# A two-layer hybrid encoder on one core: joining two 256-column products into one of 512 columns in the input projection, evicting some tiles later, and scaling the scan's outputs by priority

## The chip, the cores and the metric

The kernel runs on 1 core of one Trainium2 chip. The metric is the device time of one execution in microseconds. TensorE (PE in the profile) multiplies matrices and its weight loads are listed as PEld; VectorE is DVE, ScalarE is ACT, GpSimd is POOL, and SyncE (SP) issues most DMAs.

## The reference

Two layers, each with an RMS norm, one input projection, two groups of heads and one output projection; 256 tokens, a model width of 2048, everything in f32.

```python
for l in range(DEPTH):
    h = rms_norm(x, norm_g[l])
    proj = jnp.einsum('btd,dc->btc', h, w_in[l])
    rw_in, g_rw, q, k_at, v_at, g_at = jnp.split(proj, col_splits, axis=-1)
    rw_in = bidir_token_shift(rw_in, shift_mu[l])
    r, k, v, xw, xa = jnp.split(rw_in, rw_splits, axis=-1)
    y_rw = rwkv7_branch(r, k, v, xw, xa, ...)      # 16 heads, a scan in each direction
    ...
    y_at = window_attention(qh, kh, vh, sink[l])   # 16 heads in groups of 4, window of 128
    mix = jnp.concatenate([y_rw * jax.nn.silu(g_rw), y_at * jax.nn.silu(g_at)], axis=-1)
    x = x + jnp.einsum('btc,cd->btd', mix, w_out[l])
return rms_norm(x, final_g)
```

## The kernel before

**The products.** Each f32 operand is split into a high and a low part, and a product is the sum of three: weights high by input high, weights high by input low, weights low by input high. `gemm` computes one output tile of 128 columns of the projection for all 256 tokens. It takes 16 steps, one for each 128 rows of the model width. In the input projection a step is three matmuls with 256 moving columns each (lines 332 to 334), all added up in one PSUM tile `pm`. In the output projection (all tiles but the last) it is two: high weights by the pair (high, low) of the input, which lie side by side as 512 columns, and low weights by the high part, 256 columns (lines 325 and 326). The two halves of the 512-column result are then added when the tile is evicted.

**The weights.** A tile's weights come in two halves of 8 steps. A half is loaded from HBM into one of three `raw` buffers, then split in two pieces of 512 columns: ACT copies to `hi` (line 254) and DVE subtracts to `lo` (line 256). There are two buffers of `hi` and of `lo`, so the split of the half after next waits until PE has read the last of the half before it.

**The order of the work.** `S` is a stream of such steps in a fixed order: per layer the values, two tiles of the low-rank inputs, then eight pairs of heads with four tiles each (k, v, r and gate), then attention's 18 tiles (two of keys, eight of queries, eight of gates), then 16 output tiles. `window(64, ...)` runs 64 steps, which is one pair, and between the steps places the stages of the scans of earlier pairs (`scan_p`, `scan_i`, `scan_b`) and, in the last three windows, attention. PE's instructions stand in the order in which the code writes them. For the other engines a scheduler lists them ahead of time, by priority (the place in the code, moved by `high_priority`) and by the time at which it expects the inputs; on the chip each engine then runs its list strictly in that order. Operations written with `PV` and `PA` keep their order among themselves on DVE and ACT; those written with `V` and `A` are free.

**What the change touches.** `inproj(ct, evac)` queues one tile of the input projection, and `evac` is called when its last step has been written. `S.later(n, f)` calls `f` n steps later. `shift_evac` (lines 473 to 482) evicts k, v and r: DVE multiplies `pm` by the norm's factors `rb` into `u`, and three more operations do the token shift. `silu_evac` (lines 484 to 492) evicts a gate through two tiles of the tag `g`. `rope_evac` copies `pm` to SBUF on ACT, turns it by four DMAs and rotates it on DVE. At the first step of a pair's k tile, `ups` (lines 578 to 584) takes two tiles of the same tag `g` for two small loads (`iu`, `du`); they are read 6 steps after the eviction of that pair's v tile, by `parts` (lines 589 to 595). These two are the only buffers with the tag `g`:

```python
g = st("g", [T], bufs=2)
th = st("g", [T], bufs=2)
```

The tiles `pm` have two PSUM banks, and a tile may use a bank when the last reader of the tile that held it is done:

```python
ps_main = pool("ps_main", 2, space=PSUM)
```

In `scan_b`, at the end of a pair's scan, ACT squares the outputs, DVE forms the variance `yv` (line 1080), POOL raises it to the power -1/2 (line 1081), and DVE scales the outputs `ysq` with it.

Of the kernel before, what the change touches and what calls it, by code (L numbers as in the profile page):

```python
# [21 lines left out]
T = 256  # L22
# [3 lines left out]
NP = 8  # L26
# [34 lines left out]
WARM = 11  # L61

# [72 lines left out]
def hybrid_trunk_kernel(ctx, tc, xT, wi, wv, wo, par, fing, dup, iup, sink, pos, cst, out):  # L135
# [80 lines left out]
    def x_split(XH, XL, x, k, l):  # L216
        g = G0[:, k : k + 1] if l == 0 else PR[:, l, P_NG + k : P_NG + k + 1]
        A.activation(XH[:, k, :], x, AF.Copy, scale=g)
        V.scalar_tensor_tensor(XL[:, k, :], x, g, XH[:, k, :].bitcast(F32), op0=ALU.mult, op1=ALU.subtract)
# [90 lines left out]
    def gemm(src, operands, evac, raws=None, begin=None, bank=None, pairs=None, wide=False):  # L310
# [3 lines left out]
        def step(kk):  # L314
            def f(w):
# [7 lines left out]
                if wide:  # L323
                    m = pairs()
# [3 lines left out]
                if pairs:  # L328
                    xh, xl = (pairs().row(kk, i) for i in range(2))
                else:  # L330
                    xh, xl = (x[:, kk, :] for x in operands())
# [133 lines left out]
    def queue_inputs(l):  # L465
# [4 lines left out]
        def inproj(ct, evac, **kw):  # L470
            gemm(wi[l, ct], lambda: (L.XH, L.XL), evac, **kw)

        def shift_evac(j, place):
            def evac(pm):
                dst = place()
                u = st("u", [T], bufs=2)
                V.tensor_tensor(u, pm, L.norm.rb, op=ALU.mult)  # L477
# [6 lines left out]
        def silu_evac(place):  # L484
            def evac(pm):
                g = st("g", [T], bufs=2)
                th = st("g", [T], bufs=2)
                V.tensor_tensor(g, pm, L.norm.rb, op=ALU.mult)
# [35 lines left out]
        def v_step(kk, b):  # L524
            def f(w):
# [5 lines left out]
                PE.matmul(pvs[b], L.XH[:, kk, tb], wh, start=(kk == 0), stop=False)  # L531
                PE.matmul(pvs[b], L.XH[:, kk, tb], wl, start=False, stop=False)
                PE.matmul(pvs[b], L.XL[:, kk, tb], wh, start=False, stop=(kk == 15))
# [69 lines left out]
        for p, t in enumerate(L.ts):  # L603
            inproj(2 + 4 * p, shift_evac(p, new(t, "k", "kr", 4)), begin=ups(p, t))
            inproj(3 + 4 * p, value_evac(p, t))
            inproj(4 + 4 * p, shift_evac(16 + p, new(t, "r", "kr", 4)))
            inproj(5 + 4 * p, silu_evac(new(t, "gr", "vg", 8)))
# [4 lines left out]
        def rope_evac(place):  # L612
            def evac(pm):
# [7 lines left out]
                A.activation(raw, pm, AF.Copy)  # L621
# [13 lines left out]
                S.later(13, turn)  # L635
                S.later(15, parts)
# [12 lines left out]
        for m in range(2):  # L649
            inproj(2 + 4 * NP + m, rope_evac(k_place(m)))  # L650
# [11 lines left out]
        for n in ("q0", "q1", "q2", "q3", "g0", "q4", "g1", "q5", "g2", "q6", "g3", "q7", "g4", "g5", "g6", "g7"):  # L662
            j = int(n[1])
            if n[0] == "q":
                inproj(QG0 + 2 * j, rope_evac(q_place(j)))
            else:
                inproj(QG0 + 2 * j + 1, silu_evac(new(L.tq[j], "g", "vg", 8)))

    def queue_output(l):
# [4 lines left out]
        def tile_of(k):  # L674
# [6 lines left out]
            def evac(pm):  # L681
# [32 lines left out]
        for k in range(NKT):  # L714
            ev, be = tile_of(k)
            gemm(wo[l, k], None, ev, begin=be, pairs=lambda: L.M, wide=k < NKT - 1)

    def layer(l):
# [3 lines left out]
        L.M = Pairs()  # L722
# [294 lines left out]
        def scan_b(p, t):  # L1017
# [65 lines left out]
            PV.tensor_tensor(ysq, py, yv.unsqueeze(2).to_broadcast([128, NC, 64]), op=ALU.mult)  # L1083
# [128 lines left out]
    L0.XH, L0.XL = Rows("s2", F32R, "XH"), Rows("s3", F32R, "XL")  # L1212
    for k in range(NKT):
        x_split(L0.XH, L0.XL, X0[:, k, :], k, 0)
# [117 lines left out]
```

## Time and profile before

| | |
|---|---|
| median of 3 runs | 1160.97 us (1160.34 to 1161.03) |
| the profiled execution | 1160.44 us, of which its span is 1158.6 us |
| windows of pairs 4 to 8, layer 1 | 120.32 to 317.95 us |
| windows of attention, layer 1 | 317.95 to 488.85 us |
| windows of pairs 4 to 8, layer 2 | 689.48 to 886.18 us |
| windows of attention, layer 2 | 886.18 to 1057.12 us |

The span runs from the first to the last instruction of the profiled execution; 1.8 us of its time lie outside. A row of the timeline gives start, duration, engine, line, operation, the tiles written and read, their shape and how many instructions it merges; in brackets stand the idle time of the engine before it and what ended it. A row of the windows gives, for a stretch of time, its length and the busy time of PE, PEld, DVE, ACT and POOL with their instructions, then the granted TensorE clock, the DMA share and GB/s.

### The profile page before, as it was taken

To read this page: it belongs to the slowest core of one execution; us is meant where nothing else is said; L and a number is where in the kernel's file an instruction comes from. 1 tells how busy PE (TensorE), PEld (TensorE's weight loads), DVE (VectorE), ACT (ScalarE), POOL (GpSimd) and SP (SyncE) were. 2 spreads that over 40 slices of the span, in tenths; PEclk is the share of its full clock that TensorE was granted. 3 is DMA by queue.
4 is the path that set the end of the run, shared out by engine and by line. 5 is a ranking of instruction groups with operands and counts; after the bars stand their busy time and mean duration, and the time that the engine had idled before them with its cause. 6 is when DMAs were issued, how large, how long until landed. Compare 5 with 4: busy or idle time off the path is not lost.

```text
span 1158.6 us, 37145 instructions
## 1 busy us (share of the span) xinstructions
PE 1139.9 (98%) x15659; PEld 1046.6 (90%) x15659; DVE 914.3 (79%) x2038; ACT 783.9 (68%) x1985; POOL 22.2 (2%) x23
## 2 busy tenths in 40 slices
PE   9999999999999999999999999999999999999996
PEld 7998999999999989888999899999999999898885
DVE  7899878878977768767767898888878866786665
ACT  7687767867776667655546678767867766675553
POOL 0000000000000000000000000000000000000000
PEclk9999999999999999999999999999999999999998
DMA  7553433333334343577755444333333443336663
GB/s 276 188 174 121 136 118 99 112 118 118 111 103 132 116 124 107 151 243 235 213 184 168 143 134 139 104 118 100 112 118 112 127 123 115 119 109 198 214 195 126
DMA packets 61878, 166.73 MB, mean 144 GB/s; under 512 B 9200, under 2 KB 24208, under 8 KB 61712
## 3 DMA queue, kind: packets, MB, share of 16 engines
q1 hardware_dynamic: 61424, 164.10, 45.6%
q8 instruction: 122, 2.00, 0.7%
q14 instruction: 44, 0.36, 0.1%
q10 hardware_dynamic: 288, 0.27, 0.1%
HBM read 157.27 MB, written 4.19 MB: 139 GB/s over the span
## 4 chain that ended last, share of the span: by engine, by line
PE 74%; issue 12%; DVE 6%; ACT 4%; DMA 3%; POOL 0%; SPq 0%; POOLq 0%; DVEq 0%; ACTq 0%
PE pm L332 16%; PE pm L333 14%; PE pm L334 13%; PE pm L325 4%; PE pg L877 3%; DVE lo L256 3%; PE pm L326 2%; PE pcc L1040 2%; DMA raw<-wi 2%; PE pcc L1068 1%; PE py L1052 1%; PE pd L984 1%; PE py L1025 1%; PE pcc L1058 1%; PE pq L975 1%
## 5 line engine op out<-in xcount | busy, mean ns | idle before, releaser
L254 ACT ACTIVATE hi<-raw 128x512 fp32r<-128x512 f32 x560 | 329.8, 625 | 171.8 <-PE pm L325 61.3
L256 DVE TENSOR_TENSOR lo<-raw,hi 128x512 fp32r<-128x512 f32 x560 | 371.9, 687 | 91.1 <-ACT hi L254 88.8
L332 PE MATMUL pm<-XHa,hi 128*128 128x256 f32 x832 | 245.4, 295 | 0.0
L332 PE MATMUL pm<-XHb,hi 128*128 128x256 f32 x832 | 242.7, 292 | 0.6 <-DVE u L477 0.6
L334 PE MATMUL pm<-XHa,lo 128*128 128x256 f32 x832 | 233.8, 281 | 1.1 <-DVE lo L256 0.6
L334 PE MATMUL pm<-XHb,lo 128*128 128x256 f32 x832 | 233.3, 280 | 0.6 <-DVE lo L256 0.6
L333 PE MATMUL pm<-XLa,hi 128*128 128x256 f32 x832 | 233.3, 280 | 0.0
L333 PE MATMUL pm<-XLb,hi 128*128 128x256 f32 x832 | 233.0, 280 | 0.0
L325 PE MATMUL pm<-M,hi 128*128 128x512 f32 x480 | 166.9, 392 | 0.1
L332 PEld LDWEIGHTS pm<-XHa,hi 128*128 128x128 f32 x832 | 156.5, 188 | 10.9 <-issue 2.2
L332 PEld LDWEIGHTS pm<-XHb,hi 128*128 128x128 f32 x832 | 156.5, 188 | 6.0 <-DVE u L477 0.8
L334 PEld LDWEIGHTS pm<-XHa,lo 128*128 128x128 f32 x832 | 156.6, 188 | 2.7 <-DVE lo L256 2.5
L334 PEld LDWEIGHTS pm<-XHb,lo 128*128 128x128 f32 x832 | 156.6, 188 | 1.3 <-DVE lo L256 1.1
L333 PEld LDWEIGHTS pm<-XLa,hi 128*128 128x128 f32 x832 | 156.7, 188 | 0.0
L333 PEld LDWEIGHTS pm<-XLb,hi 128*128 128x128 f32 x832 | 156.7, 188 | 0.0
L326 PE MATMUL pm<-M,lo 128*128 128x256 f32 x480 | 134.3, 280 | 0.2 <-DVE lo L256 0.2
L325 PEld LDWEIGHTS pm<-M,hi 128*128 128x128 f32 x480 | 90.1, 188 | 20.9 <-issue 0.8
L326 PEld LDWEIGHTS pm<-M,lo 128*128 128x128 f32 x480 | 90.1, 188 | 0.5 <-DVE lo L256 0.5
L1063 ACT ACTIVATE suv<-pcc 64x128 f32<-64x128 f32 x128 | 34.5, 269 | 66.1 <-PE pcc L1061 42.4
L978 ACT ACTIVATE QF<-pq 128x256 f16<-128x256 f32 x80 | 30.4, 380 | 10.8 <-PE pq L942 6.6
L877 PE MATMUL pg<-mv,FR 64*128 64x128 f32 x512 | 37.2, 285 | 0.0
L986 DVE CAST_PREDICATED tv<-LV,pd 128x256 f16<-128x256 uint8 x80 | 34.3, 429 | 3.3 <-PE pd L984 2.7
(282 smaller groups left out, 2034.8 us busy)
## 6 DMA issues: line engine op xcount, KB each, us to landing
raw<-wi SPq DMA_DIRECT2D x208, 512.0 KB
raw<-wo SPq DMA_DIRECT2D x64, 512.0 KB
raw<-wv SPq DMA_DIRECT2D x7, 512.0 KB
rrot<-u SPq DMA_DIRECT2D x80, 32.0 KB
vg<-xT SPq DMA_DIRECT2D x16, 128.0 KB
xd<-vg SPq DMA_DIRECT2D x16, 128.0 KB
vg<-xd SPq DMA_DIRECT2D x16, 128.0 KB
g<-dup SPq DMA_DIRECT2D x16, 97.0 KB
```

Source lines behind the costliest of these rows:

```text
L254: A.activation(hi[:, q], raw[:, q], AF.Copy)
L256: V.tensor_tensor(lo[:, q], raw[:, q], hi[:, q].bitcast(F32), op=ALU.subtract)
L325: PE.matmul(pm, wh, m.row(kk), start=(kk == 0), stop=(kk == 15), skip_group_check=True)
L326: PE.matmul(pm[:, 0:T], wl, m.row(kk, 0), start=False, stop=(kk == 15), skip_group_check=True)
L332: PE.matmul(pm, wh, xh, start=(kk == 0), stop=False)
L333: PE.matmul(pm, wh, xl, start=False, stop=False)
L334: PE.matmul(pm, wl, xh, start=False, stop=(kk == 15))
L877: PE.matmul(pg[:, h, c * 128 : (c + 1) * 128], BK[half[h], d, c, 1 - h : 3 - h, :].rearrange("p s j -> p (s j)"), MV[half[h], d, c].rearra ...
L978: A.activation(t_sub(QF), flat4(pq[:, :, 0:128]), AF.Copy)
L986: V.copy_predicated(t_sub(TC), t_mask, flat4(pd[:, :, 0:128]))
L1040: PE.matmul(pc[half[h], 0, d, :], GE[h][r, d, ci[d], 0, :], SUV[r, d, ci[d], h, :], start=True, stop=True)
L1063: A.activation(here(h), pc[half[h], 1], AF.Copy)
```

## The change

The inputs `X` are laid out as pairs (high, low) as the outputs' operand already was. Attention's 18 tiles and the tiles of the pairs from the fourth on (`WIDE = 3`, counted from 0) use the two-matmul step with a `pm` of 512 columns. Evicting such a tile starts with `scaled`: ACT copies one half of `pm`, DVE adds the other, and only then comes the multiplication by `rb`; `rope_evac` gets the addition alone. `LATE` gives the steps by which the eviction of such a tile is written later in the code: 3 for k, 0 for v, 0 for r, 2 for the gate, and by turns in attention. The scaling of the scan's outputs loses its place in the fixed order of `PV`.

```diff
+LATE = (3, 0, 0, 2)
+WIDE = 3
...
                 if wide:
-                    m = pairs()
+                    m = rows()
                     PE.matmul(pm, wh, m.row(kk), start=(kk == 0), stop=(kk == 15), skip_group_check=True)
                     PE.matmul(pm[:, 0:T], wl, m.row(kk, 0), start=False, stop=(kk == 15), skip_group_check=True)
                     return
...
-        def inproj(ct, evac, **kw):
-            gemm(wi[l, ct], lambda: (L.XH, L.XL), evac, **kw)
+        def inproj(ct, evac, late=0, **kw):
+            if late:
+                evac = lambda pm, evac=evac: S.later(late, lambda: evac(pm))
+            gemm(wi[l, ct], lambda: L.X, evac, **kw)
+
+        def scaled(o, pm):
+            x = pm
+            if pm.shape[-1] > T:
+                A.activation(o, pm[:, T : 2 * T], AF.Copy)
+                V.tensor_tensor(o, o, pm[:, 0:T], op=ALU.add)
+                x = o
+            V.tensor_tensor(o, x, L.norm.rb, op=ALU.mult)
...
-                V.tensor_tensor(u, pm, L.norm.rb, op=ALU.mult)
+                scaled(u, pm)
...
-                V.tensor_tensor(g, pm, L.norm.rb, op=ALU.mult)
+                scaled(g, pm)
...
-            inproj(2 + 4 * p, shift_evac(p, new(t, "k", "kr", 4)), begin=ups(p, t))
+            inproj(2 + 4 * p, shift_evac(p, new(t, "k", "kr", 4)), begin=ups(p, t), wide=p >= WIDE, late=LATE[0] if p >= WIDE else 0)
...
-                A.activation(raw, pm, AF.Copy)
+                A.activation(raw, pm[:, T : 2 * T], AF.Copy)
+                V.tensor_tensor(raw, raw, pm[:, 0:T], op=ALU.add)
...
-                S.later(13, turn)
-                S.later(15, parts)
+                S.later(13 - late, turn)
+                S.later(15 - late, parts)
...
-            PV.tensor_tensor(ysq, py, yv.unsqueeze(2).to_broadcast([128, NC, 64]), op=ALU.mult)
+            V.tensor_tensor(ysq, py, yv.unsqueeze(2).to_broadcast([128, NC, 64]), op=ALU.mult)
```

The order of the instructions is shown at three places, all in the window of the seventh pair of layer 1; the fifth, sixth and eighth pair and layer 2 have the same pattern. Line numbers of the changed kernel are 8 to 17 higher.

PE where the k tile ends and the v tile begins, before (`pm_4523` is k, `pm_4706` is v):

```order
L332 MATMUL pm_4523<-XHb_133,hi_4609 128x256
L333 MATMUL pm_4523<-XLb_135,hi_4609 128x256
L334 MATMUL pm_4523<-XHb_133,lo_4610 128x256
L332 MATMUL pm_4706<-XHa_132,hi_4688 128x256
L333 MATMUL pm_4706<-XLa_134,hi_4688 128x256
L334 MATMUL pm_4706<-XHa_132,lo_4689 128x256
```

and now (`pm_4347` is k, `pm_4516` is v):

```order
L333 MATMUL pm_4347<-X3_135,hi_4435 128x512
L334 MATMUL pm_4347<-X3_135,lo_4436 128x256
L333 MATMUL pm_4347<-X3_135,hi_4435 128x512
L334 MATMUL pm_4347<-X3_135,lo_4436 128x256
L333 MATMUL pm_4516<-X0_132,hi_4506 128x512
```

In both, v's first matmul stands right behind k's last, with nothing of the scans between; each step has one matmul fewer now. On ACT, k's eviction now stands between the two pieces of a split:

```order
L262 ACTIVATE hi_4630<-raw_4628 128x512
L483 ACTIVATE u_4613<-pm_4347 128x256
L262 ACTIVATE hi_4630<-raw_4628 128x512
L1059 ACTIVATE rh_4524<-pcc_4519 128x128
L493 ACTIVATE kr_4612<-u_4613,DP_103 128x256
```

where before ACT had no reader of `pm` there, and both pieces stood together:

```order
L254 ACTIVATE hi_4818<-raw_4816 128x512 x2
L1042 ACTIVATE rh_4715<-pcc_4710 128x128
L478 ACTIVATE kr_4700<-u_4701,DP_103 128x256
L1000 ACTIVATE q16_4774<-pf_4721 128x512
L946 ACTIVATE tt_3776<-pf_4721 128x2x4x32
```

The copy of k's second half moved in behind the first piece of the split of v's second half.

DVE where v has ended and r begins, before:

```order
L1080 TENSOR_SCALAR yv_4909<-yv_4909 128x4
L269 TENSOR_TENSOR th_4445<-th_4445,kr_3804 128x512
L477 TENSOR_TENSOR u_4963<-pm_4706,rb_448 128x256
L269 TENSOR_TENSOR FR_493<-th_4445,ip_4601 128x8x64
L269 TENSOR_TENSOR sl_4884<-t1_4881,mf_4883 128x256
L479 SCALAR_TENSOR_TENSOR vg_4962<-u_4963,PR_83,vg_4962 128x255
L256 TENSOR_TENSOR lo_5064<-raw_5061,hi_5063 128x512
L480 SCALAR_TENSOR_TENSOR vg_4962<-u_4963,PR_83,vg_4962 128x255
L269 TENSOR_TENSOR ysq_4908<-py_4287,yv_4909 128x256
```

and now:

```order
L277 TENSOR_TENSOR th_4281<-th_4281,kr_3772 128x512
L1097 TENSOR_SCALAR yv_4714<-yv_4714 128x4
L277 TENSOR_TENSOR FR_493<-th_4281,ip_4428 128x8x64
L1100 TENSOR_TENSOR ysq_4713<-py_4133,yv_4714 128x256
L277 TENSOR_TENSOR sl_4695<-t1_4692,mf_4694 128x256
L484 TENSOR_TENSOR u_4765<-u_4765,pm_4516 128x256
```

The reading of `pm` stood two rows behind `yv`, and `ysq` eight; now `ysq` stands two rows behind `yv`, and the reading of v's `pm` behind `ysq`.

DVE where the gate of the pair before is evicted, before (`pm_4313` is that gate):

```order
L1070 TENSOR_TENSOR suv_2346<-pcc_4280,pc_2343 64x2x64 x2
L269 TENSOR_TENSOR bv_4360<-bv_4360,vg_3170 128x256
L488 TENSOR_TENSOR g_4474<-pm_4313,rb_448 128x256
L256 TENSOR_TENSOR lo_4610<-raw_4607,hi_4609 128x512
L986 COPY_PREDICATED tv_3775<-LV_104,pd_4491 128x2x8x16
```

This is fourteen rows ahead of the reading of k's `pm_4523`. Now (`pm_4159` is that gate, `iu` and `du` are split from the tiles `g_4348` and `g_4350`):

```order
L277 TENSOR_TENSOR iu_4850<-g_4348,iuh_4849 96x256
L277 TENSOR_TENSOR du_4854<-g_4350,duh_4853 97x256
L1003 COPY_PREDICATED tv_4492<-LV_104,pd_4871 128x2x32x4
L264 TENSOR_TENSOR lo_4982<-raw_4979,hi_4981 128x512
L484 TENSOR_TENSOR g_4354<-g_4354,pm_4159 128x256
```

The gate's eviction moved from ahead of the reading of the next k tile to behind the reading of the next v tile and behind the split of `iu` and `du`, whose raw tiles were taken ahead of `g_4354`.

More of the change, by code (lines that the diff above doesn't have):

```diff
@@ L308, in hybrid_trunk_kernel, with gemm @@
     S = Stream()
-    def gemm(src, operands, evac, raws=None, begin=None, bank=None, pairs=None, wide=False):
+    def gemm(src, rows, evac, raws=None, begin=None, bank=None, wide=False):
         box = []
@@ L327, in f @@
                     return
[L328 to L331, printed above, removed]
+                xh, xl = (rows().row(kk, i) for i in range(2))
                 PE.matmul(pm, wh, xh, start=(kk == 0), stop=False)
@@ L530, in f @@
                 tb = slice(b * 128, (b + 1) * 128)
-                PE.matmul(pvs[b], L.XH[:, kk, tb], wh, start=(kk == 0), stop=False)
-                PE.matmul(pvs[b], L.XH[:, kk, tb], wl, start=False, stop=False)
-                PE.matmul(pvs[b], L.XL[:, kk, tb], wh, start=False, stop=(kk == 15))
+                PE.matmul(pvs[b], L.X.row(kk, 0)[:, tb], wh, start=(kk == 0), stop=False)
+                PE.matmul(pvs[b], L.X.row(kk, 0)[:, tb], wl, start=False, stop=False)
+                PE.matmul(pvs[b], L.X.row(kk, 1)[:, tb], wh, start=False, stop=(kk == 15))
             return f
@@ L649, in queue_inputs @@
         for m in range(2):
-            inproj(2 + 4 * NP + m, rope_evac(k_place(m)))
+            inproj(2 + 4 * NP + m, rope_evac(k_place(m), LATE[m]), late=LATE[m], wide=True)
         L.tq = [dict() for _ in range(8)]
@@ L660, in q_place @@
             return place
-        for n in ("q0", "q1", "q2", "q3", "g0", "q4", "g1", "q5", "g2", "q6", "g3", "q7", "g4", "g5", "g6", "g7"):
+        for i, n in enumerate(("q0", "q1", "q2", "q3", "g0", "q4", "g1", "q5", "g2", "q6", "g3", "q7", "g4", "g5", "g6", "g7")):
             j = int(n[1])
+            late = LATE[(i + 2) % 4]
             if n[0] == "q":
-                inproj(QG0 + 2 * j, rope_evac(q_place(j)))
+                inproj(QG0 + 2 * j, rope_evac(q_place(j), late), late=late, wide=True)
             else:
-                inproj(QG0 + 2 * j + 1, silu_evac(new(L.tq[j], "g", "vg", 8)))
+                inproj(QG0 + 2 * j + 1, silu_evac(new(L.tq[j], "g", "vg", 8)), late=late, wide=True)
     def queue_output(l):
@@ L715, in queue_output @@
             ev, be = tile_of(k)
-            gemm(wo[l, k], None, ev, begin=be, pairs=lambda: L.M, wide=k < NKT - 1)
+            gemm(wo[l, k], lambda: L.M, ev, begin=be, wide=k < NKT - 1)
     def layer(l):
@@ L1211, in hybrid_trunk_kernel @@
     L0.norm = Norm()
[L1212 removed]
+    L0.X = x_rows()
     for k in range(NKT):
[L1214 removed]
+        x_split(L0.X, X0[:, k, :], k, 0)
         S.run(2)
```

33 lines of the change are left out of this document (19 added, 14 removed).

## The prediction

> **What bounds the kernel now.** I read the page's first part, then the windows by stage, to see which engine has no time left where the change is made.
>
> ```profile
> PE 1139.9 (98%) x15659; PEld 1046.6 (90%) x15659; DVE 914.3 (79%) x2038; ACT 783.9 (68%) x1985; POOL 22.2 (2%) x23
> ...
> 120.32:317.95 197.63, 197.12 (x3668) 182.71 (x3667) 169.36 (x353) 149.56 (x396) 5.32 (x4) 1.00 0.37 114
> 317.95:488.85 170.90, 170.59 (x2516) 154.80 (x2515) 129.51 (x355) 115.40 (x336) 4.39 (x4) 1.00 0.40 120
> 689.48:886.18 196.70, 196.68 (x3668) 182.52 (x3666) 169.10 (x352) 149.35 (x396) 5.26 (x4) 1.00 0.37 115
> ```
>
> In the pairs' windows PE is idle for 0.51 of 197.63 us and for 0.02 of 196.70 us, in attention's for 0.31 of 170.90 us. DVE has 14% to spare with the pairs and 24% in attention. So PE's own rate sets the time: what shortens a PE step is gained whole, and any wait newly put before a PE instruction is lost whole, since nothing on PE is slack.
>
> **The joined product.** The starts of matmuls, uninterrupted, in three narrow runs and a wide one of the output stage:
>
> ```profile
> 602.84 0.28 PE L332 MATMUL pm<-XHa,hi 128*128 128x256 f32 x1
> ...
> 618.85 0.28 PE L332 MATMUL pm<-XHb,hi 128*128 128x256 f32 x1
> ...
> 302.67 0.28 PE L332 MATMUL pm<-XHb,hi 128*128 128x256 f32 x1
> ...
> 304.08 0.28 PE L332 MATMUL pm<-XHb,hi 128*128 128x256 f32 x1
> ...
> 32.93 0.28 PE L332 MATMUL pm<-XHb,hi 128*128 128x256 f32 x1
> ...
> 49.83 0.28 PE L332 MATMUL pm<-XHb,hi 128*128 128x256 f32 x1
> ...
> 540.12 0.39 PE L325 MATMUL pm<-M,hi 128*128 128x512 f32 x1
> ...
> 545.66 0.39 PE L325 MATMUL pm<-M,hi 128*128 128x512 f32 x1
> ```
>
> The first run has 45 steps in 16.01 us, 355.8 ns each; the second, in a pair's window, 4 steps in 1.41 us, 352.5 ns; the third 48 steps in 16.90 us, 352.1 ns; the wide one 16 steps in 5.54 us, 346.3 ns. A wide step therefore saves 5.8 to 9.5 ns; I take 6.2, from the run in the window that changes. Wide become 5 pairs x 4 tiles and 18 tiles of attention, 38 tiles x 16 steps x 2 layers = 1216 steps: -7.5 us, between -7.1 and -11.6.
>
> A page of the Trainium skill gives another size: "TensorE: Matmul & The Clock Gate", section "Wait — 56ns, not 53.3ns?", says that a warm matmul follows the one before after its columns at 2.4 GHz and some 2.5 ns, so a joined pair would save 2.5 ns, and 1216 of them about 3.0 us, an estimate by that page. The rows here do not agree (a lone 256-column matmul takes 117 ns by the second run, not 109), and by the page the forecast below would be 4.5 us later.
>
> **The longer eviction.** The copy and the addition have these counterparts:
>
> ```profile
> L621 ACT ACTIVATE u<-pm 128x256 f32<-128x256 f32 x20 | 7.5, 376 | 0.0
> L685 DVE TENSOR_TENSOR vg<-pm,vg 128x256 f32<-128x256 f32 x16 | 6.8, 424 | 13.3 <-PE pm L326 12.4 <-PE pm L334 0.9
> ```
>
> DVE gets 76 additions (38 tiles, 2 layers) of 0.42 us, 32 us; ACT gets 56 copies of 0.38 us, 21 us (the rotary tiles were copied before). By stage that is 20 x 0.42 = 8.4 us for DVE with a layer's pairs, from 169.4 to 178 of 197.6 us, and 18 x 0.42 = 7.6 us in attention, from 129.5 to 137 of 170.9. As load this is covered by the idle time of both engines: 0 us, at most what one addition in each pair tile would cost if every one fell into a PE wait, 40 x 0.42 = 17 us. I take 0, since the idle time left is still 20 us a layer. Attention's four DMAs per rotary tile leave up to one addition and 3 steps (1.04 us) later, while the rotation stays at the same step; DVE already waits for such DMAs, which costs PE nothing visible in the 0.31 us above. I take 0 there too. On SP the weights keep their order, and only some small loads at the start of the outputs change places; POOL's eight powers per layer stay, but what waits for them changes, which comes below.
>
> **Where the eviction stands on PE's path.** This decides the case. Before, two PSUM banks alternate, and a tile's bank has long been read when its turn comes. In a window of the pairs:
>
> ```profile
> 236.29 0.42 DVE L488 TENSOR_TENSOR g<-pm,rb 128x256 f32<-128x256 f32 x1 [1.30 <-PE pm L334]
> ...
> 238.12 0.38 PE L332 MATMUL pm<-XHa,hi 128*128 128x256 f32 x1
> ...
> 263.96 0.42 DVE L269 TENSOR_TENSOR iu<-g,iuh 96x256 fp32r<-96x256 f32 x1
> 264.31 0.41 DVE L269 TENSOR_TENSOR du<-g,duh 97x256 fp32r<-97x256 f32 x1
> ```
>
> The gate is read at 236.29 us, before the next pair's k tile begins at 238.12. Its eviction is now written 2 steps into that k tile, behind `ups`, which has just taken both `g` buffers. They come free when `iu` and `du` are split, at about 264 us here, after k and v have ended. The order of DVE says the same: the gate's `pm` is read behind v's. So one bank stays with the gate while k and v are computed. v must use the bank that k has just filled, and r the bank of v. PE cannot start v before both readers of k are done, nor r before those of v, and behind that first matmul the whole PE queue waits, the scans' products too. It happens where a wide gate is followed by a pair: fifth to eighth pair, 4 windows x 2 layers, twice in each. In attention no `ups` follows, and the banks alternate.
>
> From k to v the present rows give the wait:
>
> ```profile
> 247.48 0.28 PE L334 MATMUL pm<-XHb,lo 128*128 128x256 f32 x1
> 247.60 0.28 PE L332 MATMUL pm<-XHa,hi 128*128 128x256 f32 x1
> ...
> 247.73 1.15 ACT L254 ACTIVATE hi<-raw 128x512 fp32r<-128x512 f32 x2 [1.08 <-issue]
> ...
> 247.80 0.42 DVE L477 TENSOR_TENSOR u<-pm,rb 128x256 f32<-128x256 f32 x1 [0.85 <-PE pm L334]
> 248.39 1.29 DVE L256 TENSOR_TENSOR lo<-raw,hi 128x512 fp32r<-128x512 f32 x2 [0.17 <-ACT hi L254]
> ```
>
> k's last matmul starts at 247.48, ends at 247.76, and a waiting reader starts 0.04 us after that, at 247.80; v starts at 247.60. In the new order ACT first splits a piece whose buffer k's last weights held (from 247.73, half of 1.15 us), then copies, 248.31 to 248.68; DVE first does that piece's `lo` (from 248.39; the next instruction can follow 1.29 - 0.68 = 0.61 us later), then adds, 249.00 to 249.42. With another 0.04 us v starts at 249.46 in place of 247.60: 1.86 us lost. Without the two pieces ahead it would be the copy from 247.80 to 248.18, the addition from 248.22 to 248.64, v at 248.68: 1.08 us.
>
> From v to r the scan's output stands ahead:
>
> ```profile
> 257.07 0.28 PE L334 MATMUL pm<-XHb,lo 128*128 128x256 f32 x1
> 257.19 0.28 PE L332 MATMUL pm<-XHa,hi 128*128 128x256 f32 x1
> ...
> 257.35 0.17 DVE L1080 TENSOR_SCALAR yv<-yv 128x4 f32<-128x4 f32 x1
> ...
> 337.28 0.16 DVE L1080 TENSOR_SCALAR yv<-yv 128x4 f32<-128x4 f32 x1
> 337.40 0.69 DVE L269 TENSOR_TENSOR FR<-th,ip 128x512 f32<-128x512 f32 x1
> 338.99 0.42 DVE L269 TENSOR_TENSOR ysq<-py,yv 128x256 f32<-128x256 f32 x1 [0.90 <-POOL yv L1081]
> 339.33 0.68 DVE L256 TENSOR_TENSOR lo<-raw,hi 128x512 fp32r<-128x512 f32 x1
> ```
>
> At 337 us the present kernel has the new order once (`yv`, `FR`, `ysq`): `ysq` starts 1.71 us after `yv`, held by POOL, and the next instruction 0.34 us later. `yv` falls at 257.35, so `ysq` at 259.06, `sl` at 259.40, the addition at 259.74 to 260.16, and r at 260.20 in place of 257.19: 3.01 us lost. If `yv` came early enough not to matter, it would be 1.86 as above. So the freed place of `ysq` is no gain: DVE's queue now waits for POOL right ahead of an addition for which PE waits.
>
> Sum: 8 x (1.86 + 3.01) = 39.0 us, between 8 x (1.08 + 1.86) = 23.5 and, with one more 0.61 us instruction ahead in each, 48.8 us. While PE stands, DVE and ACT catch up, a further reason for the 0 above.
>
> **The time.** 1160.44 (the profiled execution) - 7.5 + 39.0 = 1191.9 us; the median shown is 0.5 us above the profiled one, so 1192.5 us.
>
> **The rivals.**
> - Faster: the eviction ends before PE comes, and only the joined product counts. 1161.0 - 7.5 = 1153.5 us. It would need a loss under 7.5 / 16 = 0.47 us at each of the 16 places. For it speaks that DVE and ACT are free at 247.7 (idle 0.85 and 1.08 us before); against it that the copy and the addition alone take 0.80 us. Chance 0.06; 0.03 more for something near the time before.
> - A lower price: neither split nor POOL stands in the way, 23.5 us. 1160.97 - 7.5 + 23.5 = 1177 us. For it: the scheduler put them there by its own clock, and the order of arrival may differ; against it: the lists are run in order. Chance 0.16.
> - The clock falls. These rows show what a pause does:
>
> ```profile
> 645.00:650.00 5.00, 3.35 (x26) 2.94 (x25) 4.93 (x10) 3.36 (x9) 0.00 (x0) 1.00 0.53 175
> ...
> 1148.70:1151.00 2.30, 1.23 (x4) 0.93 (x4) 0.91 (x2) 0.00 (x0) 0.08 (x1) 0.50 0.00 0
> ...
> 1145.95 0.28 PE L334 MATMUL pm<-M,lo 128*128 128x256 f32 x1
> ...
> 1.22 4.51 PE L1209 MATMUL warm<-QF 128*128 128x512 f16 x11 [1.22 <-DVE QF L1204]
> ```
>
> At the end the granted clock is 0.50 from 1148.7 us, 2.8 us after the last dense matmul; at 645 us PE paused 1.65 of 5 us and the clock stayed at 1.00. A pause of 3.0 us lies beyond the first of these. At the start, eleven 512-column matmuls take 4.51 us, 0.41 each where 0.23 is the full rate (346.3 - 117), so a restart loses some 2 us; after each of 8 pauses that is 16 us: 1208 us. Chance 0.14.
>
> On this the same page of the Trainium skill, in its section "What's actually happening", says that the clock halves after an idle window of about 3.4 us and returns after a busy one; the pause from v to r would stay just under it, and with the few matmuls in the window it would not count. The end of this trace is nearer than that page, a drop after 2.8 us with a few small matmuls between, which is why the rival keeps its chance.
>
> **How the numbers follow.** The forecast has 0.61 (1184 to 1202 us by itself), the clock 0.14, the lower price 0.16, faster 0.06, near the old time 0.03. The range for 8 in 10 reaches from the lower price, 1176, to just below the clock's case, 1206. About 0.2% is what a measurement of this kernel can tell from no change: faster 0.06, same 0.03, slower 0.91.
>
> **What would show it.** In the trace after: PE waits for DVE at the first matmul of v and r in the pairs' windows, 16 times, about 1.9 and 3.0 us long; these two windows' stages grow by some 17 us each, attention's shrink by about 2 us; wide steps near 346 ns; `ysq` waits for POOL at eight more places; PEclk 1.00. It would be wrong if PE's waits at those places were under half a microsecond, or if the gate's `pm` were read before v ends.

## The result: 6% slower, 38 us beyond the forecast

| | median | range of runs |
|---|---|---|
| before | 1160.65 us | 1159.62 to 1161.03 |
| after | 1230.85 us | 1230.05 to 1232.41 |

The ratio is 1.0607, 95% interval 1.0595 to 1.0620. The forecast was 1192.5 us with a range to 1206. The direction and the place were right; the size was not. The profiled execution of the changed kernel took 1230.05 us, its span 1228.3. Executions in a slower state, over 1.5% above the fastest of the same kernel, are left out of every time below.

From the page of the changed kernel, the row of PE's busy time and the row of the granted clock in 40 slices of the span:

```profile
PE 1159.5 (94%) x14443; PEld 992.4 (81%) x14443; DVE 940.5 (77%) x2114; ACT 800.7 (65%) x2041; POOL 22.5 (2%) x23
...
PEclk9999998898899999999999999898898999999998
```

Before, PE was busy 98% of the span and stood for 19 us; now it stands for 69 us, and the clock dips in the slices of the pairs of both layers. The windows by stage (length, then busy time of PE, PEld, DVE, ACT and POOL, the granted clock, the DMA share and GB/s) are pairs 4 to 8 and then attention, layer 1 and layer 2:

```profile
120.06:351.24 231.18, 209.60 (x3349) 173.61 (x3347) 176.57 (x371) 155.53 (x415) 5.53 (x4) 0.93 0.32 97
351.24:525.97 174.73, 168.97 (x2229) 137.66 (x2227) 134.77 (x373) 117.80 (x345) 4.33 (x4) 1.00 0.38 116
725.96:955.38 229.42, 208.17 (x3349) 172.41 (x3347) 176.20 (x370) 155.53 (x415) 5.47 (x4) 0.94 0.32 98
955.38:1127.26 171.88, 168.94 (x2228) 137.70 (x2226) 133.90 (x369) 117.58 (x345) 4.33 (x4) 1.00 0.38 118
```

Against the rows of before the pairs grew by 33.6 and 32.7 us, attention by 3.8 and 0.9 us, although each should have shrunk by the joined product's gain. The waits of PE (engine, tile and line that waited, what it waited for; us in total, times, the longest):

```profile
PE pm L333 <- DVE u L484: 41.0, 16, 3.6
PE pm L334 <- DVE lo L264: 2.9, 4, 0.9
```

The first row is the forecast's mechanism: 16 waits of a tile's first matmul for the addition in the eviction (line 484). The bank is held as forecast, too: in the seventh pair of layer 1 the gate of the pair before is read at 287.95 us, behind `iu` and `du` and 8 us after r has begun.

```profile
285.67 0.42 DVE L277 TENSOR_TENSOR iu<-g,iuh 96x256 fp32r<-96x256 f32 x1 [2.76 <-ACT iuh L277]
286.01 0.41 DVE L277 TENSOR_TENSOR du<-g,duh 97x256 fp32r<-97x256 f32 x1
...
287.95 0.42 DVE L484 TENSOR_TENSOR g<-g,pm 128x256 f32<-128x256 f32 x1
```

The timeline of the seventh pair of layer 1 at both places, k to v first:

```profile
265.55 0.36 ACT L483 ACTIVATE u<-pm 128x256 f32<-128x256 f32 x1
...
265.68 0.69 DVE L264 TENSOR_TENSOR lo<-raw,hi 128x512 fp32r<-128x512 f32 x1 [1.40 <-ACT hi L262]
266.28 0.42 DVE L484 TENSOR_TENSOR u<-u,pm 128x256 f32<-128x256 f32 x1
...
266.75 0.51 PE L333 MATMUL pm<-X,hi 128*128 128x512 f32 x1 [1.71 <-DVE u L484]
...
276.22 0.28 PE L334 MATMUL pm<-X,lo 128*128 128x256 f32 x1
...
277.05 0.16 DVE L1097 TENSOR_SCALAR yv<-yv 128x4 f32<-128x4 f32 x1
277.17 0.69 DVE L277 TENSOR_TENSOR FR<-th,ip 128x512 f32<-128x512 f32 x1
278.76 0.42 DVE L1100 TENSOR_TENSOR ysq<-py,yv 128x256 f32<-128x256 f32 x1 [0.90 <-POOL yv L1098]
279.10 0.42 DVE L277 TENSOR_TENSOR sl<-t,mf 128x256 fp32r<-128x256 f32 x1
279.43 0.41 DVE L484 TENSOR_TENSOR u<-u,pm 128x256 f32<-128x256 f32 x1
...
279.90 0.80 PE L333 MATMUL pm<-X,hi 128*128 128x512 f32 x1 [3.40 <-DVE u L484]
```

From k to v the order of the forecast stands: a `lo`, the addition, then v. From v to r the addition waits behind `yv`, `FR`, `ysq` and `sl`, and `ysq` waits 0.90 us for POOL. r could have started 0.12 us after 276.22, at 276.34, and started at 279.90: 3.56 us lost. The addition's end then frees PE at half speed: the first matmul of r takes 0.80 us in place of 0.51. The windows on both sides of that start, in steps of 3.41 us:

```profile
275.80:279.21 3.41, 0.70 (x5) 0.34 (x3) 2.51 (x7) 2.82 (x13) 1.37 (x1) 1.00 0.43 133
279.21:282.62 3.41, 2.72 (x58) 2.19 (x60) 3.38 (x9) 0.47 (x2) 0.00 (x0) 0.50 0.10 32
282.62:286.04 3.42, 3.42 (x23) 2.88 (x16) 0.66 (x3) 3.24 (x13) 0.00 (x0) 0.50 0.43 141
286.04:289.45 3.41, 3.41 (x53) 2.80 (x52) 2.77 (x9) 2.75 (x7) 0.00 (x0) 1.00 0.03 7
```

The granted clock is 0.50 from 279.21 to 286.04 us, 6.83 us, though PE works again from 279.90. This happens after each of the eight pauses before r. A ninth fall, of one window, follows a pause from k to v, in the fifth pair of layer 1:

```profile
166.57:169.99 3.42, 1.71 (x18) 1.10 (x18) 2.02 (x5) 1.42 (x3) 0.00 (x0) 1.00 0.48 156
169.99:173.40 3.41, 3.41 (x89) 2.97 (x84) 2.50 (x7) 1.54 (x4) 0.00 (x0) 0.50 0.52 156
```

### The profile page after: what moved, and what is told of

Read it like the earlier page. It is cut to its first block, busy times and chain, and to the rows that moved or that the text cites. A ratio compares the mean times of both kernels' runs of the same rounds, so it can differ in the third digit from the quotient of the medians.

```text
span 1228.3 us, 34819 instructions
## 1 busy us (share of the span) xinstructions
PE 1159.5 (94%) x14443; PEld 992.4 (81%) x14443; DVE 940.5 (77%) x2114; ACT 800.7 (65%) x2041; POOL 22.5 (2%) x23
## 4 chain that ended last, share of the span: by engine, by line
PE 62%; issue 13%; DVE 11%; ACT 8%; DMA 3%; POOL 1%; SPq 1%; DVEq 0%; POOLq 0%; ACTq 0%
PE pm L333 23%; PE pm L334 11%; DVE lo L264 4%; PE pm L337 3%; PE pg L894 3%; PE pm L339 3%; PE pm L338 3%; ACT hi L262 2%; PE pcc L1057 1%; DMA raw<-wi 1%; POOL yv L1098 1%; PE py L1069 1%; PE pcc L1085 1%; PE pd L1001 1%; PE pcc L1075 1%
## 5 line engine op out<-in xcount | busy, mean ns | idle before, releaser
L333 PE MATMUL pm<-X,hi 128*128 128x512 f32 x1216 | 469.7, 421 | 41.0 <-DVE u L484 41.0
L262 ACT ACTIVATE hi<-raw 128x512 fp32r<-128x512 f32 x560 | 334.8, 626 | 177.6 <-PE pm L333 76.0
L334 PE MATMUL pm<-X,lo 128*128 128x256 f32 x1216 | 347.4, 286 | 2.9 <-DVE lo L264 2.9
L333 PEld LDWEIGHTS pm<-X,hi 128*128 128x128 f32 x1216 | 236.0, 194 | 105.6 <-DVE u L484 46.0
L334 PEld LDWEIGHTS pm<-X,lo 128*128 128x128 f32 x1216 | 237.3, 195 | 4.2 <-DVE lo L264 4.2
L337 PE MATMUL pm<-X,hi 128*128 128x256 f32 x448 | 128.1, 286 | 0.6 <-DVE u L486 0.6
L339 PE MATMUL pm<-X,lo 128*128 128x256 f32 x448 | 126.5, 282 | 1.6 <-DVE lo L264 1.2
L338 PE MATMUL pm<-X,hi 128*128 128x256 f32 x448 | 125.6, 280 | 0.0
L339 PEld LDWEIGHTS pm<-X,lo 128*128 128x128 f32 x448 | 84.3, 188 | 3.5 <-DVE lo L264 3.5
L337 PEld LDWEIGHTS pm<-X,hi 128*128 128x128 f32 x448 | 84.4, 188 | 2.0 <-DVE u L486 0.8
L338 PEld LDWEIGHTS pm<-X,hi 128*128 128x128 f32 x448 | 84.4, 188 | 0.0
L1098 POOL TENSOR_TENSOR yv<-yv,mhalf 128x4 f32<-128x4 f32 x16 | 19.7, 1229 | 915.1 <-DVE yv L1097 915.1
L1163 ACT ACTIVATE mv<-mv,mx 128x257 f32<-128x257 f32 x56 | 27.9, 501 | 11.3 <-DVE mx L1160 11.1
```

Of the source, the lines that this page charges most:

```text
L262: A.activation(hi[:, q], raw[:, q], AF.Copy)
L333: PE.matmul(pm, wh, m.row(kk), start=(kk == 0), stop=(kk == 15), skip_group_check=True)
L334: PE.matmul(pm[:, 0:T], wl, m.row(kk, 0), start=False, stop=(kk == 15), skip_group_check=True)
L337: PE.matmul(pm, wh, xh, start=(kk == 0), stop=False)
L338: PE.matmul(pm, wh, xl, start=False, stop=False)
L339: PE.matmul(pm, wl, xh, start=False, stop=(kk == 15))
```

## The experiments

All times stand against the kernel before, run on the same chip beside them (1160.0 to 1160.5 us). Where windows are compared, it is the window of the seventh pair of layer 1, from the first matmul of its k tile to that of the eighth pair's. In the kernel before and after it reads:

```profile
238.12:278.04 39.92, 39.92 (x753) 37.08 (x751) 34.04 (x72) 30.42 (x82) 1.31 (x1) 1.00 0.36 112
```

```profile
255.54:303.40 47.86, 42.75 (x689) 35.42 (x687) 35.72 (x76) 31.72 (x86) 1.37 (x1) 0.93 0.30 94
```

### What holds the bank: three runs

**The gate read at once.**

```diff
-LATE = (3, 0, 0, 2)
+LATE = (3, 0, 0, 0)
```

> Only the gate's eviction goes back to the step at which its tile ends (LATE's fourth number 2 becomes 0); everything else is as in the changed kernel (1230.9 us). Theory A (the gate's eviction, written behind the next pair's small loads, gets no g buffer until those are done, so its PSUM bank stays taken and v and r stand in banks that are just being read; the pauses also halve the clock): all 16 waits of PE for the addition of the longer eviction go, 43.4 us, and the clock stays at 1.00, some 24 us more: 1230.9 - 43.4 - 24 = 1163 us, down to 1153 us if the smaller stalls in attention go with them. Theory B (the longer eviction as such, a copy and an addition more for ACT and DVE, is what PE waits for, wherever the gate is read): the 16 waits stay, about 1230 us. Theory C (the k tile's eviction, 3 steps late, holds v up): the eight waits before v stay at 1.9 us and only those before r may change: about 1180 to 1195 us.

Measured: 1172.56 us, ratio 1.0101 (1.0086 to 1.0116). The 16 waits are gone and the clock stays at 1.00. The largest wait of PE that is left, and the window:

```profile
PE pm L334 <- DVE lo L264: 9.6, 13, 1.3
```

```profile
239.85:280.36 40.51, 39.80 (x688) 33.28 (x687) 35.13 (x76) 32.00 (x86) 1.37 (x1) 1.00 0.36 111
```

58 of the 70 us go with one number of the change. But 12 us remain, 9.6 more than theory A's 1163 us leave. The largest wait is now for the lower parts of weights, 9.6 us in 13 waits (2.9 us in 4 in the changed kernel); with the scaling in another place, below, it falls back to some 3 us.

**The small loads later.**

```diff
 def ups(p, t):
     def begin():
         ...
-    return begin
+    return lambda: S.later(2, begin)
```

> The gate's eviction stays 2 steps late, but the next pair's small loads, which take both g buffers, are written 2 steps later as well, so behind it. Theory A (it is the order in which the g buffers are taken, not the lateness, that keeps the bank): the 16 waits go and the clock stays at 1.00, 1153 to 1163 us, equal to the run with the gate read at once. Theory B (the longer eviction as such) and theory D (the gate's lateness by itself, because DVE is then busy with it when k ends): about 1230 us, or at least the eight waits before v, 8 x 1.87 = 15 us above the run with the gate read at once.

Measured: 1171.67 us, 1.0096 (1.0081 to 1.0111), the same as the run before, and the 16 waits are gone. The gate's eviction is written as late as in the changed kernel, so it is not this lateness in the code that holds the bank, but the order in which the two `g` buffers are taken. The reading itself is not late here, though. The addition that reads the gate's `pm`, in the run before and in this one:

```profile
239.67 0.41 DVE L484 TENSOR_TENSOR g<-g,pm 128x256 f32<-128x256 f32 x1
```

```profile
239.43 0.41 DVE L484 TENSOR_TENSOR g<-g,pm 128x256 f32<-128x256 f32 x1
```

The seventh pair's k tile begins at 239.85 and 239.60 us, so both runs read the gate just ahead of it. With the buffers free, DVE's list has the addition at the same place, wherever the code writes it. What a gate that is really read two steps late would cost (theory D) no run shows.

**The k tile at once, the gate late.**

```diff
-LATE = (3, 0, 0, 2)
+LATE = (0, 0, 0, 2)
```

> The changed kernel with the k tile's eviction at once (LATE's first number 3 becomes 0) and the gate's still 2 steps late. Theory A (the gate's bank is what is held): v still stands in the bank that k has just filled and r in that of v, so 16 waits stay, those before v of 1.9 us and those before r of 3.6 us, with the halved clock: 1225 to 1235 us. Theory C (the lateness of the k tile's eviction is at fault): the waits go, 1165 to 1195 us.

Measured: 1233.19 us, 1.0622 (1.0603 to 1.0641). The first row of its waits is that of the changed kernel but for 0.1 us in the longest:

```profile
PE pm L333 <- DVE u L484: 41.0, 16, 3.7
```

Theory C falls: the later k is not at fault.

### POOL's wait and the clock: two runs

**The scaling behind the addition.**

```diff
-V.tensor_tensor(ysq, py, yv..., op=ALU.mult)
+with tc.high_priority(offset=-400):
+    V.tensor_tensor(ysq, py, yv..., op=ALU.mult)
```

> The banks stand as in the changed kernel, so PE still waits 16 times; only the scaling of the scan's output, which waits for POOL's power, is put behind the value tile's addition on DVE. Theory A with POOL's wait as the reason why v to r costs more than k to v: v to r falls from 3.56 to about 1.9 us lost, 8 x 1.7 = 13.5 us; and since pauses of 1.9 us before v leave the clock at 1.00, the eight stretches at 0.50 go too, some 24 us: 1230.9 - 13.5 - 24 = 1193 us, which is what the prediction's sum had. Rival E (the halved clock is not a cost of its own, or does not come from these pauses): 1217 us. Rival F (POOL is not what holds the addition): 1231 us.

Measured: 1216.09 us, 1.0485 (1.0467 to 1.0502), between the theories. The start of the sixth pair's r tile, and the clock around it:

```profile
226.46 0.50 PE L333 MATMUL pm<-X,hi 128*128 128x512 f32 x1 [2.06 <-DVE u L484]
```

```profile
223.75:227.16 3.41, 1.35 (x8) 0.91 (x6) 3.41 (x9) 2.75 (x12) 1.36 (x1) 1.00 0.38 133
227.16:230.57 3.41, 3.41 (x63) 2.81 (x62) 2.60 (x7) 2.38 (x11) 0.00 (x0) 0.50 0.38 141
```

The wait fell from 3.40 to 2.06 us, so POOL's share of a pause was 1.34 us, 10.7 us in all; `FR` and `sl` stay ahead of the addition, which is why it is not 1.7. The clock did not stay up, though theory A had it so: a pause of 2.06 us, in a window where PE was busy 1.35 of 3.41 us, still halves it, now for one window in place of two. After two of the pauses from k to v, 1.71 us, it falls as well.

**PE kept busy in the pause.** Twelve matmuls of 512 columns, whose results are not used, stand between v's last matmul and r's first in the fifth to eighth pair.

```diff
+if kk == 0 and fill:
+    w_ = wbank("fill")
+    for _ in range(fill):
+        PE.matmul(w_, BONES, rows().row(0), start=True, stop=True)
```

> The changed kernel with 12 more 512-column matmuls of unused results on PE between v's last matmul and r's first, in the fifth to eighth pair: about 12 x 0.23 = 2.75 us of work inside the pause of 3.6 us. Where PE's wait comes from is left as it is. Theory A with the clock as a separate cost set by PE's idleness: the clock stays at 1.00, the pause itself stays (or is 0.1 to 0.3 us longer), 1230.9 - 24 = 1207 us. Rival E (the halved clock costs nothing of its own, or follows from something else than PE standing idle): 1231 us or a little more.

Measured: 1214.66 us, 1.0463 (1.0441 to 1.0484). The run's seventh pair, r's start, and the windows of the r tile and of the gate's tile:

```profile
271.09 2.97 PE L332 MATMUL fill<-X,BONES 128*128 128x512 f32 x12
274.65 0.50 PE L337 MATMUL pm<-X,hi 128*128 128x512 f32 x1 [0.60 <-DVE u L488]
```

```profile
274.65:284.09 9.44, 9.44 (x178) 7.93 (x179) 7.43 (x19) 7.93 (x25) 0.00 (x0) 1.00 0.19 59
284.09:295.73 11.64, 11.62 (x172) 9.59 (x170) 10.54 (x23) 8.61 (x22) 0.00 (x0) 1.00 0.52 155
```

And the same two tiles in the changed kernel:

```profile
279.90:292.04 12.14, 12.14 (x178) 10.08 (x179) 8.71 (x22) 8.76 (x27) 0.00 (x0) 0.75 0.17 54
292.04:303.40 11.36, 11.36 (x173) 9.59 (x171) 9.49 (x20) 7.88 (x20) 0.00 (x0) 1.00 0.50 149
```

The pause lasts as long as before (r starts 3.56 us after the first of the twelve), but the r tile takes 9.44 us in place of 12.14. The gate's tile takes 0.28 us more, so a halved clock costs 12.14 - 9.44 - 0.28 = 2.4 us, eight times 19 us. This is a cost of its own beside the wait. The whole run gained 16 us, not 19: after four of the pauses from k to v, which are not filled, the clock fell for one step of 3.41 us, at 1.5 us each, where the changed kernel has one such fall. Theory A's mechanism stands, at a lower price than its 24 us.

### Where the other 12 us come from: copies, attention, scaling

**Without the second half.** The gate at once, and the wide tiles are evicted from their first 256 columns alone.

```diff
-A.activation(o, pm[:, T : 2 * T], AF.Copy)
-V.tensor_tensor(o, o, pm[:, 0:T], op=ALU.add)
-x = o
+x = pm[:, 0:T]
...
```

> As the run with the gate read at once (1172.6 us), but the wide tiles are evicted from their first 256 columns alone, in one instruction as before the change: the copy on ACT and the addition on DVE are left out, and with them the product with x's lower part, from the result. Theory G (the 12 us that this run still lies over the kernel before are the price of the copies and additions, which put DVE and ACT behind where they split weights and feed the scan): only the joined product is left, 1216 steps x 6.6 ns = 8 us, 1160.3 - 8.0 = 1152.3 us; in the fifth to eighth pair a window falls from 40.5 to 39.5 us. Theory H (the 512-column steps themselves bring the waits, since PE consumes weights faster and the order of the instructions on the engines has changed): 1165 to 1172 us. Theory I (the joined product saves nothing in the stage): 1160 us.

Measured: 1160.27 us, 1.000 (0.999 to 1.001). By the number that is theory I, but the same eviction with the scaling in a better place, the last run below, shows the joined product's gain in the stage.

**The copy without the addition.**

```diff
 A.activation(o, pm[:, T : 2 * T], AF.Copy)
-V.tensor_tensor(o, o, pm[:, 0:T], op=ALU.add)
...
```

The rotary tiles lose theirs likewise.

> As the run with the gate read at once (1172.6 us), but the wide tiles are evicted from their last 256 columns alone, with ACT's copy and without DVE's addition (the product with x's first part is left out of the result). Theory G1 (of the two added instructions DVE's costs, since the weights' lower parts that PE waited for are split on DVE): 1152 to 1156 us. Theory G2 (ACT's copy costs as much, since scan products wait for ACT): 1160 to 1168 us. Theory H (neither): 1170 to 1173 us.

Measured: 1162.63 us, 1.0018 (1.0009 to 1.0028). By the number that is theory G2, but beside the run before it the parts are told apart: taking the additions away gives 9.9 us, the copies 2.4 us more, so of the two DVE's part is the larger. Theory G is half right: with nothing added, the joined product's 8 us did not appear. Something else cost as much.

**Attention alone.**

```diff
-WIDE = 3
+WIDE = 8
```

> Only the 18 wide tiles of attention per layer are kept (WIDE = 8, no pair is wide), with the lateness of the changed kernel there. The prediction's sum gives them 18 x 16 x 2 x 6.6 ns = 3.8 us of gain and nothing lost: 1156.5 us. The changed kernel's trace gives by stage +1.2 us in the window of the keys and first queries, and +2.6 us and -0.4 us in the two layers' attention, so 1160.3 + 2 x 1.2 + 2.6 - 0.4 = 1165 us. If those losses were carried over from the pairs' backlog on DVE, 1157 to 1160 us. No wait at the pairs' value and receptance tiles in any case, and the clock at 1.00.

Measured: 1172.81 us, 1.0103 (1.0085 to 1.0120), a miss by more than 7 us. The pairs, which are narrow here, grew to 41.3 us a window. Their wait:

```profile
PE pd L1001 <- ACT tt L963: 16.2, 16, 1.3
```

Two parts of the change are left in the pairs' windows, the layout of X and the scaling. The next run has the scaling alone.

**The scaling alone**, in the kernel before:

```diff
-PV.tensor_tensor(ysq, py, yv..., op=ALU.mult)
+V.tensor_tensor(ysq, py, yv..., op=ALU.mult)
```

> The kernel before with one word of the change: the scan's outputs are scaled by priority (V in place of PV). No product is wide and nothing is late. Theory J (the scaling by priority is a cost of its own: it stands two places behind the variance on DVE, DVE is idle 0.90 us for POOL's power, and the scan's chain FR, QF, tt behind it comes late for PE, 1.4 us in each of the fifth to eighth pair's windows, as in the run with attention alone): 1160.0 + 8 x 1.4 = 1171 us. Theory K (the run with attention alone was slow because of the new layout of X or of attention's DMAs, and the scaling costs nothing because DVE has 14% to spare): 1160 to 1162 us.

Measured: 1170.27 us, 1.0088 (1.0074 to 1.0103), within a microsecond of theory J's 1171 us. DVE, then ACT and PE, in the sixth pair's window:

```profile
217.25 0.17 DVE L1080 TENSOR_SCALAR yv<-yv 128x4 f32<-128x4 f32 x1
217.33 0.68 DVE L269 TENSOR_TENSOR th<-th,kr 128x512 f32<-128x512 f32 x1
218.91 0.42 DVE L1083 TENSOR_TENSOR ysq<-py,yv 128x256 f32<-128x256 f32 x1 [0.90 <-POOL yv L1081]
219.25 0.68 DVE L269 TENSOR_TENSOR FR<-th,ip 128x512 f32<-128x512 f32 x1
...
219.97 0.63 ACT L269 ACTIVATE FR<-FR 64x512 f32<-64x512 f32 x1 [1.54 <-DVE FR L269]
...
222.43 0.30 PE L984 MATMUL pd<-QF,tt 64*64 64x32 f16 x16 [1.28 <-ACT tt L946]
```

DVE stands 0.90 us for POOL, `FR` behind it is late, ACT waits 1.54 us for `FR` with `QF` and `tt` queued behind, and PE waits 1.28 us for `tt`. One instruction moved forward on an engine with idle time costs 10 us.

**Attention alone, the scaling in its turn**: `WIDE = 8` with `PV`.

> As the run with attention alone, with the scaling in its turn (PV). Theory J: the windows of the pairs fall from 41.3 to the 39.9 us of before and the ninth from 40.06 to 38.8 or less, and attention keeps its gain of 1152 ns a layer or so: 1172.8 - 8 x 1.4 - 2 x 1.2 - 2 = 1157 to 1160 us. Theory K (layout or attention's DMAs): 1170 us or more.

Measured: 1159.36 us, 0.9992 (0.9984 to 1.0001). It agrees with theory J: 13.5 us go with the one word. Of the 3.8 us that attention's joined tiles should give, 0.8 are left, which is no measurable gain.

**The gate at once, the scaling in its turn.**

> The changed kernel with the gate read at once and the scaling in its turn again (PV); joined products and the later k stay. Theory J: the 1.0 us by which the fifth to eighth pair's windows lie over the joined product's gain goes, 40.5 to 39.5 us, and in the ninth window 1.2 us: 1172.6 - 8 x 1.0 - 2 x 1.2 = 1162 us, and 1157 us or less if attention's stalls go with them, down to 1152 us, the joined product's gain alone. Theory G (copies and additions are the price of the 12 us): 1168 to 1173 us.

Measured: 1176.20 us, 1.0133 (1.0118 to 1.0147): a miss, and slower than with the scaling early. DVE and PE in the sixth pair's window:

```profile
225.36 0.48 DVE L495 SCALAR_TENSOR_TENSOR vg<-u,PR,vg 128x255 f32<-128x255 f32 x1
225.76 0.41 DVE L277 TENSOR_TENSOR ysq<-py,yv 128x256 f32<-128x256 f32 x1
...
226.23 0.68 PE L1105 MATMUL py<-C,ysq 64*64 64x64 f32 x16 [1.46 <-DVE ysq L277]
```

In its turn, the scaling now stands behind the whole longer eviction of a wide tile, and PE waits for it. There are eight such waits, 12.4 us, the longest 2.2. After two of them, one of 2.19 us and one of 1.46, the clock falls for one window, which by the 1.5 us of a fall above is about 3 us; the run with the gate at once has no such fall. Theory J is right on the narrow kernel, but with wide tiles neither place is good.

**All at once, the scaling in its turn**: all of `LATE` is 0, with `PV`.

> As the run with the gate at once and the scaling in its turn, and the k tile's eviction is not late either (all of LATE is 0). If the lateness of k and of attention's first tiles helps DVE through the places where it splits weights, this is 1 to 5 us slower than that run; if the lateness only shifts the burst, it is the same within 1 us; if it hurts, 1 to 3 us faster, which would be the fastest version so far, some 1152 to 1157 us.

Measured: 1177.75 us, 1.0141 (1.0125 to 1.0157). Against the run before it the intervals overlap, and the profiled execution has four falls of the clock against two; the lateness of k is worth nothing that can be told.

### A place between

**The scaling between**, with the gate at once:

```diff
-V.tensor_tensor(ysq, py, yv..., op=ALU.mult)
+if p < 4:
+    with tc.high_priority(offset=-100):
+        V.tensor_tensor(ysq, py, yv..., op=ALU.mult)
+else:
+    PV.tensor_tensor(ysq, py, yv..., op=ALU.mult)
```

> The run with the gate read at once, but in the fifth to eighth pair's windows the scaling of the scan's outputs stands 4 places behind the variance on DVE (2 places with V, 9 with PV), and in the later windows in its turn. Theory L (only the place is at fault: early, DVE idles 0.9 us for POOL and all behind it is late; late, PE waits 1.6 us for the scaled outputs): both waits go, the fifth to eighth pair's windows fall from 40.5 (V) and 41.2 (PV) to 39.5 us each, 1172.6 - 8 x 1.0 - 2 x 0.8 (ninth window 39.25) - 2 = 1161 us, down to 1156 us. Theory G (the copies and additions load DVE so that something is late wherever the scaling stands): windows of 40 us or more, 1165 to 1173 us.

Measured: 1162.49 us, 1.0016 (1.0007 to 1.0025), 1.5 us above theory L's 1161 and under theory G's 1165. The scaling waits 0.23 us for POOL in place of 0.90, and the window:

```profile
219.46 0.42 DVE L1102 TENSOR_TENSOR ysq<-py,yv 128x256 f32<-128x256 f32 x1 [0.23 <-POOL yv L1098]
```

```profile
238.06:277.88 39.82, 39.78 (x689) 33.28 (x687) 35.11 (x76) 31.78 (x86) 1.37 (x1) 1.00 0.37 113
```

**The same from the fifth pair on** (`WIDE = 4`).

> As the run with the scaling between, with the wide tiles from the fifth pair on (WIDE = 4). The fourth pair's window was 37.85 us with wide tiles and 37.05 us before, where PE waits 1.2 us once for the lower part of a weight: 2 x 0.8 = 1.6 us less than that run. If that wait only moves to the fifth pair's window, the same time.

Measured: 1158.03 us, 0.9979 (0.9969 to 0.9988), the fastest version with the whole product: 2.4 us under the kernel before. The gain over the previous run, 4.5 us, is more than the 1.6 expected. Its DVE is at 81%, as in that run; the fourth pair's windows gave 1.4 us of it, and the rest lies in attention of layer 1 (132.8 to 130.9 us) and in smaller pieces.

**Between, without the second half.**

> As the run with the scaling between, but the wide tiles are evicted from their first 256 columns alone, without the copy on ACT and the addition on DVE; the product with x's lower part is left out of the result. It gives what the joined product is worth when nothing is added and the scaling stands well. Theory L: 39.5 us in the fifth to eighth pair's windows and 1152 to 1156 us in all (1160.1 - 8.0 = 1152), at most 3 us under the run with the scaling between. Theory G: the same 1152 to 1156 us, but 8 us or more under that run. If the joined product gives nothing here, 1160 us.

Measured: 1155.77 us, 0.9958 (0.9945 to 0.9971). Its window has no idle time on PE at all:

```profile
235.43:274.97 39.54, 39.54 (x688) 33.29 (x687) 33.87 (x72) 30.41 (x82) 1.01 (x1) 1.00 0.36 114
```

Against 39.92 us before, that is 0.38 us for 64 steps, 5.9 ns a step. With the copies and additions (39.82 us) 0.28 us of the 0.38 go again. So theory L holds in these windows, and part of theory G for the rest of the kernel: the two runs differ by 6.7 us, more than the 3 us that L allowed and less than G's 8: 2.9 us in the fifth to eighth pair's windows, 2.6 in the fourth's (37.85 against 36.52 us and 37.83 against 36.53) and 1.8 in attention of layer 1, with 1.7 us the other way in the ninth; the rest is spread.

## Why the prediction failed, step by step

- **PE bounds the kernel, and any new wait is lost whole.** Right: the 16 waits are found again in the windows' time, as the sum below shows.
- **The joined product, -7.5 us.** Right as a rate: 5.9 ns a step measured, 6.2 taken. The Trainium skill's 2.5 ns ("TensorE: Matmul & The Clock Gate", section "Wait — 56ns, not 53.3ns?") would have made that window 0.16 us shorter; 0.38 was measured. As a sum it is kept only where nothing else moves; attention's share came to 0.8 us.
- **The held bank: 16 waits by the order of the `g` buffers.** Right, shown by the row that reads the gate behind `iu` and `du`, by the two runs that free the bank and by the one that leaves only the pair's gate late.
- **k to v, 1.86 us.** Measured: 1.87 us (266.75 us against a start that was due at 264.88, 0.12 us behind k's last matmul).
- **v to r, 3.01 us.** Measured: 3.56. The mechanism was right, and POOL's part was 1.34 us. The working took `yv` as 0.16 us later than r's due start; it came 0.71 us later, behind two `lo` and a `th`. Eight times 0.55 us is 4.4 us.
- **The clock.** This step failed, and it carries 19 of the 38 us missing. The sum put the clock at nothing; it was a rival at 0.14, priced at 2 us a pause (2.4 measured), and the forecast rested on a pause of 3.0 us staying under the threshold. The rows quoted for it bracketed the threshold (1.65 of 5 us idle: no fall; 2.8 us after the last dense matmul: a fall), and 3.0 us lay outside the bracket on the side of the fall. Nor was 2.8 us of idleness needed there. The last window at full clock in the kernel before has PE busy for more than half of it:

```profile
1145.28:1148.69 3.41, 1.90 (x17) 1.72 (x15) 0.58 (x2) 0.92 (x2) 0.61 (x1) 1.00 0.00 0
```

The Trainium skill's section "What's actually happening" ("TensorE: Matmul & The Clock Gate") was set against the fall at the end as a reason to doubt it; the run with the scaling behind shows that a full idle window isn't needed.
- **DVE's and ACT's load, 0 us.** Wrong. Idle time as a share (14% on DVE) doesn't cover an instruction that lands in a burst: taking the copies and additions out of the run with the scaling between gives 6.7 us, the most per window in the fourth pair's (1.3 us).
- **The scaling's new place.** Half wrong: the wait for POOL was seen, but priced only where the addition stood behind it. What else stood behind it, `FR`, `QF` and `tt`, feeds PE too; alone that is 10 us. With the gate's bank held, the wait for POOL is part of the pause (1.34 us of it); what it costs without the pause shows once the bank is free.
- **Attention's DMAs, 0 us.** Nothing shows a cost of the DMAs themselves. Attention and the ninth windows still grew by 4.8 us together where -3.6 was forecast; some 3.7 of it goes in the run with the gate at once and the scaling in its turn.

In sum for one window of the fifth to eighth pair: 1.87 + 3.56 + 2.4 - 0.38 = 7.45 of the measured 47.86 - 39.92 = 7.94 us. The remaining half microsecond is not told apart; DVE's and ACT's load (0.28 us a window by the last two windows above) and the scaling's new place are what is left for it. Eight windows give 64 us; the fourth pair's windows add 1.6 and the ninth's and attention's 4.8, together 70 us. Of the 38 us that the forecast lacks, the clock is 19, the longer wait before r 4, attention and the ninth windows 8 and the fourth pair's 2; most of the rest is that half microsecond, eight times.

What stays open: why attention of layer 1 takes 2 to 5 us more than that of layer 2 in some of these kernels, and whether a version with the attention tiles narrow would beat the fastest one here; no run settles either.

## What to carry to other kernels

When an eviction is moved later, look at every buffer that it allocates and at who allocates the same tag in between: a PSUM bank is held by the reader's other buffers as much as by the reader. Before an instruction that waits for a slow engine is moved forward on a busy queue, list what stands behind it and who waits for each of those; of the three places tried here, 4 instructions behind its producer was better than 2 and 9. And a pause of TensorE can have a second price, the clock behind it: in these traces the pauses of 2 us and more between matmuls of the pairs all did, those of 1.5 to 1.7 us at some places and not at others.

## What the runs showed of the hardware

The granted clock changes in steps of 3.41 us. A window in which PE was busy 0.70 of 3.41 us was followed by two windows at 0.50, one with 1.35 of 3.41 us by one. How many follow is not set by that alone: in the run with the k tile at once, 0.77 us (788.21 to 791.62) was followed by one, through the whole of which PE was busy.

Where a pause falls bears on whether it counts. The pause from k to v lasts 1.71 us each time. In the fifth pair of layer 1 of the changed kernel it lay whole in one window, which left 1.71 us busy, and the clock fell (the rows of 166.57 us above). In the seventh pair it lay across a border, which left 2.22 us, and the clock stayed:

```profile
265.56:268.97 3.41, 2.22 (x89) 1.84 (x90) 2.42 (x5) 1.80 (x6) 0.00 (x0) 1.00 0.49 144
268.97:272.38 3.41, 3.41 (x66) 2.89 (x67) 3.33 (x8) 1.16 (x4) 0.00 (x0) 1.00 0.36 141
```

So the limit lies between 1.71 and 2.22 us busy in a window, by these rows. It is not sharp in PE's busy time as the profile has it: 1.70 us in the run with PE kept busy (165.95 to 169.36) and 1.82 us in the changed kernel (681.99 to 685.40) were followed by no fall, 1.95 us in the run with the gate at once and the scaling in its turn (758.42 to 761.83, around a pause of 1.46 us) by one. The Trainium skill ("TensorE: Matmul & The Clock Gate", section "What's actually happening") has the window's length, about 3.4 us, and that it runs freely; the trace agrees with both. It speaks of an idle window; here one that was half busy was enough.
